# A gated, two-branch attention layer on one core: the down-projection as seven block products instead of eight

## The chip, the cores and the metric

The kernel runs on one core of one Trainium2 chip. The time is that of one execution on the device, in microseconds (us); it is given as the median of three runs, and one further execution was recorded by the profiler.

## The reference

One layer (DEPTH = 1) of 1024 positions by 1024 channels, all in float32. Two attention branches, gates and an output projection come first; none of them is touched here. The change lies in the channel mixing and in the last normalisation:

```python
h = _layer_norm(x) * (1.0 + sc2) + sh2
u = _causal_depthwise_conv(h @ w_up[l], conv_w[l], conv_b[l])   # (1024, 2 * 2816)
a, val = jnp.split(u, 2, axis=-1)
y = (jax.nn.silu(a) * val) @ w_down[l]                          # (1024, 2816) @ (2816, 1024)
x = _layer_norm(alpha * x + (1.0 + g2) * y, ln2_g[l], ln2_b[l])
```

## The kernel before

**Precision.** Each float32 operand of a large product is split in a high part, rounded to the multiplication format fp32r, and a low part, the rest. A product is then three matmuls: high by high, high by low, low by high. ScalarE (ACT) casts the high part, and GpSimd (POOL) or VectorE (DVE) subtracts to get the low part. So an operand of 128x512 costs a cast and a subtraction beside its loads.

**Up-projection** (`up(c)`, once for each of 22 blocks of 128 hidden channels). The up-projection is already done with seven block products instead of eight: the 1024 positions are two halves, the 1024 input channels two halves, and each block has one weight block of the gate and one of the value. Sums and differences of weights (`s1`, `s2`, `wt`, L1015, L1017, L727, on DVE) meet sums and differences of the input that were formed earlier; `product` (L741) issues 12 matmuls into a PSUM bank, and the results are combined by ACT copies and by DVE additions (`add`, L995). Some banks (`main`, `side`) are added to again by the next product after they have been read. The first eight blocks have two of their products done ahead of time (`early`, five products left); they alternate with later blocks in `order`. `conv` makes the causal convolution in PSUM (L976 on ACT, L978 twice on DVE), then SiLU (L981, ACT) and the product with the value (L983, DVE), which gives `y`, the block's 128 channels by 1024 positions. `stored()` at the next block's start writes `y` to the DRAM tensor `yd`.

**Down-projection.** The 1024 positions are taken in two halves of four row tiles; the 1024 output columns are two halves of 512. For a half of positions eight PSUM banks hold the sums (4 row tiles by 2 column halves), and for each of the 22 blocks `down` issues 4 x 2 x 3 matmuls. `load_g` fetches a half of `yd` (256 KB) and splits it (L1067 on ACT, L1068 on DVE; on POOL for the first three); `load_down` fetches 128 rows of `w_down` (512 KB) and splits them (L1061 on ACT, L1062 on POOL). The split weights of 16 blocks stay in SBUF for the second half of positions, those of six blocks are loaded and split again. The first three blocks (`FIRST`) are prepared in the up-projection's own buffers, before its memory is given over to the pool `dn`. In the second half the last six blocks (`LAST`) are taken row tile by row tile, so that a row tile is finished while the next ones are multiplied.

**Last normalisation.** `residual_2` multiplies a bank with `g2row` (`z`, L1120) and adds the scaled residual (L1121); `finish` takes the statistics (L115, L117 and some one-column instructions), normalises on ACT (L136), multiplies with `l2g` on DVE (L1127; on POOL for row tile 6), adds `l2b` on POOL (L1128) and stores. Row tile 7 is done in two halves on DVE alone (L1134, L1135), with no ACT and no POOL.

**Order.** The program is written as one stream; a scheduler places the instructions into the queues of the engines with its own model of time, waits included. Each engine then serves its queue strictly in order. Nearly all loads and stores are issued from one queue, that of SyncE (SP). Buffers of a pool are reused in turn: an instruction that writes a buffer waits for the last reader of what lay there.

Of the kernel before, what the change touches and what calls it, by code (L numbers as in the profile page):

```python
# [11 lines left out]
F32 = mybir.dt.float32  # L12
# [30 lines left out]
def body(ctx, tc, a, out):  # L43
# [41 lines left out]
    yd = dram.tile([NFF, P, S], F32, name="yd", tag="yd")  # L85
# [26 lines left out]
    def norm_scale(src, n=2):  # L112
        st = small.tile([P, n, 6], F32, name=nm("st"), tag=f"st{n}", bufs=4 if n == 2 else 1)
        for i in range(n):
            ve.bn_stats(out=st[:, i, :], in_=src[:, i * D // n : (i + 1) * D // n])  # L115
# [15 lines left out]
    def normalise(dst, src, on_act=False):  # L131
        mv, r = norm_scale(src)
        if on_act:
            b = small.tile([P, 1], F32, name=nm("nb"), tag="nb")
            ve.scalar_tensor_tensor(out=b, in0=mv[:, 0:1], scalar=-1.0, in1=r, op0=ALU.mult, op1=ALU.mult)
            se.activation(out=dst, in_=src, func=AF.Identity, scale=r, bias=b)  # L136
        else:
            ve.tensor_scalar(out=dst, in0=src, scalar1=mv[:, 0:1], scalar2=r, op0=ALU.subtract, op1=ALU.mult)
# [848 lines left out]
    def stored():  # L987
        while pending:
            c, ya = pending.pop()
            sy.dma_start(out=yd[c], in_=ya)  # L990
# [6 lines left out]
    def up(c):  # L997
# [60 lines left out]
    def load_down(dh, dl, c):  # L1058
        st = wp.tile([P, D], F32, name=nm("ws"), tag="ws")
        sy.dma_start(out=st, in_=a["w_down"][order[c]])  # L1060
        se.copy(out=dh, in_=st)  # L1061
        po.tensor_sub(out=dl, in0=st, in1=dh)  # L1062
        return dh, dl

    def load_g(st, gh, gl, c, half, eng):
        sy.dma_start(out=st, in_=yd[order[c], :, halves(half)])
        se.copy(out=gh, in_=st)  # L1067
        eng.tensor_sub(out=gl, in0=st, in1=gh)  # L1068
        return gh, gl

    def down(ps, t, g, d, start, stop, ns=(0, 1)):
        ts = slice(t * P, (t + 1) * P)
        for n in ns:
            pe.matmul(ps[n], g[0][:, ts], d[0][:, halves(n)], start=start, stop=False)  # L1074
            pe.matmul(ps[n], g[0][:, ts], d[1][:, halves(n)], start=False, stop=False)  # L1075
            pe.matmul(ps[n], g[1][:, ts], d[0][:, halves(n)], start=False, stop=stop)  # L1076

    def banks():
        return [[(mxt if t == 3 else mxp).tile([P, H], F32, name=nm("psd"), tag="tt" if t == 3 else "mm") for _ in range(2)]
                for t in range(4)]  # L1080

    ps = banks()
    firsts = []
    for c in range(FIRST):
        w = slot([P, 2, H], F32R)
        g = load_g(hbp.tile([P, H], F32, name=nm("gs"), tag="fs", bufs=2), w[:, 0], w[:, 1], c, 0, po)
        firsts.append((g, load_down(slot([P, D], F32R), slot([P, D], F32R), c)))
    stored()
    for c in range(FIRST):
        for t in range(4):  # L1090
            down(ps[t], t, *firsts[c], c == 0, False)
# [5 lines left out]
    with tc.tile_pool(name="dn", bufs=2, reuse_waits="tile") as dn:  # L1097
        downs = {}
        fixed = [FIRST + 2, FIRST + 3]

        def next_down(c):
            if c in fixed:
                dh, dl = [wp.tile([P, D], F32R, name=nm("dd"), tag=tag) for tag in ("wh", "wl")]
            else:
                d = dn.tile([P, 2, D], F32R, name=nm("dd"), tag="dd", bufs=KEEP)
                dh, dl = d[:, 0], d[:, 1]
            downs[c] = load_down(dh, dl, c)

        def next_g(c, half):
            return load_g(dn.tile([P, H], F32, name=nm("gs"), tag="gs", bufs=2),  # L1110
                          dn.tile([P, H], F32R, name=nm("gh"), tag="gh", bufs=LAST + 1),
                          dn.tile([P, H], F32R, name=nm("gl"), tag="gl", bufs=LAST + 1), c, half, ve)

        def residual_2(t, ps, w=H):
            y = dn.tile([P, D], F32, name=nm("yt"), tag="yt", bufs=4)
            sy.dma_start(out=y, in_=xd[t])
            for n in range(D // w):
                ns = slice(n * w, (n + 1) * w)
                z = dn.tile([P, w], F32, name=nm("z"), tag="z", bufs=2)
                ve.tensor_tensor(out=z, in0=ps[n * w // H][:, n * w % H : n * w % H + w], in1=g2row[:, ns], op=ALU.mult)  # L1120
                ve.scalar_tensor_tensor(out=y[:, ns], in0=y[:, ns], scalar=ALPHA, in1=z, op0=ALU.mult, op1=ALU.add)  # L1121
            return y

        def finish(t, y):
            if t < NT - 1:
                normalise(y, y, True)
                (po if t == NT - 2 else ve).tensor_tensor(out=y, in0=y, in1=l2g, op=ALU.mult)  # L1127
                po.tensor_tensor(out=y, in0=y, in1=l2b, op=ALU.add)  # L1128
# [8 lines left out]

        for c in range(FIRST, NFF):
            next_down(c)
            g = next_g(c, 0)  # L1140
            for t in range(4):
                down(ps[t], t, g, downs[c], False, c == NFF - 1)
        l2g = dn.tile([P, D], F32, name="l2g", tag="l2g", bufs=1)
        l2b = dn.tile([P, D], F32, name="l2b", tag="l2b", bufs=1)
        sy.dma_start(out=l2g, in_=a["ln2_g"].partition_broadcast(P))
        sy.dma_start(out=l2b, in_=a["ln2_b"].partition_broadcast(P))
        ys = [residual_2(t, ps[t]) for t in range(4)]
        ring = [c for c in range(FIRST, NFF) if c not in fixed]
        kept = ring[-KEEP:]
        again = list(range(FIRST)) + ring[:-KEEP]  # L1150
        turn = kept[: len(again)] + fixed + kept[len(again) : KEEP - LAST] + again + kept[KEEP - LAST :]
        ps = banks()
        for i, c in enumerate(turn[:-LAST]):
            if c in again:
                next_down(c)
            g = next_g(c, 1)
            for t in range(4):
                down(ps[t], t, g, downs[c], i == 0, False)
            if i < 4:
                finish(i, ys[i])  # L1160
        gs = [next_g(c, 1) for c in turn[-LAST:]]
        for t in range(4):
            for ns in ((0, 1),) if t < 3 else ((0,), (1,)):
                for i, c in enumerate(turn[-LAST:]):
                    down(ps[t], t, gs[i], downs[c], False, i == LAST - 1, ns)
            finish(4 + t, residual_2(4 + t, ps[t], H if t < 3 else H // 2))
# [64 lines left out]
```

## Time and profile before

| | |
|---|---|
| three runs | 1646.95, 1649.61, 1650.62 us; median 1649.61 |
| the profiled execution | 1647.35 us, of which the span from its first to its last instruction 1645.6 |
| TensorE (PE) busy | 1564.6 us, 95% of the span |
| VectorE (DVE) busy | 1078.8 us, 66% |
| ScalarE (ACT) busy | 780.1 us, 47% |
| GpSimd (POOL) busy | 540.5 us, 33% |
| mean granted TensorE clock | 0.982 of full speed |
| up-projection | until 1392 us |
| down-projection | 1392 to 1632 us |
| after the last matmul | to 1645.6 us |

Instructions are named by the kernel's line (L741), engine, operation and tiles, output before inputs (`psu<-hc,wx`). Busy time of PE is modelled and doesn't show how full its pipeline is. An idle time is put down to what ended it (`<-ACT gh L1067`). In the timeline, a row has its start, its length from the first start to the last end, the engine and line, and how many instructions are merged in it.

### The profile page before, as it was taken

The page shows a single profiled execution, that of the slowest core. Times are in us where ns is not written, and L with a number is a line of the kernel's source. Part 1 is how long each engine was busy: PE and PEld are TensorE (multiplying, and loading weights), DVE is VectorE, ACT ScalarE, POOL GpSimd, SP SyncE. Part 2 cuts the span into 40 slices and gives each one's busy share as a digit, 9 for nine tenths or more (in the row PEclk, how much of TensorE's full clock was granted, in tenths as well). Part 3 has the DMA queues.
Part 4 walks back from the last instruction along what each step waited for, and adds up shares of the span by engine and source line. Part 5 has one row for each costly group of instructions (what it writes and reads, how often), then busy time and mean ns, then how long its engine had stood idle before and what let it go on. Part 6 is the DMA issues. An engine that isn't in the chain of part 4 may idle for free. (4 is left out here: it accounts for less than half of the span.)

```text
span 1645.6 us, 21971 instructions
## 1 busy us (share of the span) xinstructions
PE 1564.6 (95%) x7821; PEld 1301.3 (79%) x7821; DVE 1078.8 (66%) x2189; ACT 780.1 (47%) x1380; POOL 540.5 (33%) x516
## 2 busy tenths in 40 slices
PE   6899999999999999999998969999999999999996
PEld 3788888889888888877876757788888888888885
DVE  6738776686677665537598795767766664554617
ACT  3547556655565555654245363444454454331311
POOL 1111213112322322222063544544444444550602
PEclk9999999999999999999998989999999999999998
DMA  9134432342252333247446245323332212761611
GB/s 348 43 95 120 139 91 77 114 129 65 77 167 84 103 96 122 72 163 245 153 161 236 97 159 165 116 97 119 113 101 97 77 71 90 246 215 45 204 40 51
DMA packets 81823, 205.80 MB, mean 125 GB/s; under 512 B 8561, under 2 KB 17329, under 8 KB 81713
## 3 DMA queue, kind: packets, MB, share of 16 engines
q1 hardware_dynamic: 77104, 197.49, 37.0%
q10 hardware_dynamic: 4608, 6.90, 1.1%
q8 instruction: 61, 1.00, 0.3%
q14 instruction: 50, 0.40, 0.1%
HBM read 157.14 MB, written 38.83 MB: 119 GB/s over the span
## 5 line engine op out<-in xcount | busy, mean ns | idle before, releaser
L98 POOL TENSOR_TENSOR wl<-ws,wh 128x1024 fp32r<-128x1024 f32 x54 | 133.0, 2466 | 320.1 <-ACT wh L97 293.6
L741 PE MATMUL psu<-hc,wx 128*128 128x512 f32 x804 | 194.9, 397 | 4.0 <-DVE u L995 4.0
L741 PEld LDWEIGHTS psu<-hc,wx 128*128 128x128 f32 x804 | 151.9, 189 | 41.4 <-DVE u L995 4.8
L978 DVE SCALAR_TENSOR_TENSOR pcv<-u,convp,pcv 128x1024 f32<-128x1024 f32 x88 | 113.0, 1284 | 48.2 <-ACT pcv L976 47.6
L1068 DVE TENSOR_TENSOR gl<-gs,gh 128x512 fp32r<-128x512 f32 x41 | 64.2, 1572 | 102.3 <-ACT gh L1067 94.5
L1074 PE MATMUL psd<-dd,gh 128*128 128x512 f32 x328 | 127.6, 389 | 0.0
L1075 PE MATMUL psd<-dd,gh 128*128 128x512 f32 x328 | 127.6, 389 | 0.0
L1076 PE MATMUL psd<-dd,gl 128*128 128x512 f32 x328 | 127.4, 389 | 0.0
L459 ACT ACTIVATE s<-s,mx 128x640 f32<-128x640 f32 (+7 forms) x128 | 94.6, 739 | 47.5 <-DVE mx L453 46.0
L498 ACT CAST pt<-pst 128x512 fp32r<-128x512 f32 (+1 forms) x192 | 82.4, 452 | 67.4 <-PE pst L494 63.4
L211 PE MATMUL psq<-h1h,wh 128*128 128x512 f32 x256 | 104.7, 410 | 2.0 <-DVE h1h L207 2.0
L211 PE MATMUL psg<-h1h,wh 128*128 128x512 f32 x256 | 103.9, 406 | 0.0
L212 PE MATMUL psq<-h1l,wh 128*128 128x512 f32 x256 | 101.1, 395 | 0.0
L213 PE MATMUL psq<-h1h,wl 128*128 128x512 f32 x256 | 100.9, 394 | 0.0
L499 DVE TENSOR_TENSOR pt<-pst,pt 128x512 fp32r<-128x512 f32 (+1 forms) x192 | 96.7, 517 | 5.9 <-ACT pt L498 4.0
L212 PE MATMUL psg<-h1l,wh 128*128 128x512 f32 x256 | 100.2, 392 | 0.0
L213 PE MATMUL psg<-h1h,wl 128*128 128x512 f32 x256 | 100.2, 391 | 0.0
L509 PE MATMUL pso<-pt,vs 128*128 128x256 f32 x608 | 92.0, 290 | 3.5 <-DVE o L514 1.7
L509 PEld LDWEIGHTS pso<-pt,vs 128*128 128x128 f32 x608 | 81.8, 191 | 12.9 <-ACT pt L498 4.0
L1062 POOL TENSOR_TENSOR dd<-ws,dd 128x1024 fp32r<-128x1024 f32 x25 | 62.5, 2504 | 89.3 <-ACT dd L1061 86.0
L97 ACT CAST wh<-ws 128x1024 fp32r<-128x1024 f32 x54 | 56.4, 1047 | 67.6 <-PE psq L212 20.6
L494 PE MATMUL pst<-ident,s 128*128 128x128 f32 x528 | 81.7, 273 | 7.1 <-DVE pt L499 3.7
(245 smaller groups left out, 4009.9 us busy)
## 6 DMA issues: line engine op xcount, KB each, us to landing
ws<-in_w_up SPq DMA_DIRECT2D x52, 512.0 KB, 3.4
wa<-in_w_ada SPq DMA_DIRECT2D x64, 256.0 KB, 3.1
ws<-in_w_down SPq DMA_DIRECT2D x28, 512.0 KB, 3.5
yd<-y SPq DMA_DIRECT2D x22, 512.0 KB, 3.0
gs<-yd SPq DMA_DIRECT2D x44, 256.0 KB, 3.5
wa<-in_w_ada SPq DMA_DIRECT2D x8, 1024.0 KB, 12.1
ws<-in_w_qk SPq DMA_DIRECT2D x16, 512.0 KB, 5.0
ws<-in_w_g SPq DMA_DIRECT2D x16, 512.0 KB, 3.7
```

Of the source, the lines that this page charges most:

```text
L98: po.tensor_sub(out=lo, in0=st, in1=hi)
L211: pe.matmul(ps, wh, xh, start=start, stop=False)
L212: pe.matmul(ps, wh, xl, start=False, stop=False)
L213: pe.matmul(ps, wl, xh, start=False, stop=stop)
L459: se.activation(out=st[:, 0:nk], in_=st[:, 0:nk], func=AF.Exp, scale=-1.0, bias=prev, accum_out=sm)
L499: ve.tensor_sub(out=dl, in0=src, in1=dh)
L509: pe.matmul(ps[:, 0:256], vs[:, j0 + j, :], pt[c][j // 4][:, j % 4, :], start=j == 0 and c == 0, stop=j == nj - 1 and c == 1)
L741: pe.matmul(ps, w[:, a_, k, :], h[k][b_], start=first, stop=k == 3 and a_ == 1, skip_group_check=on)
L978: ve.scalar_tensor_tensor(out=ps, in0=u[b][:, 2 - d : S + 2 - d], scalar=cp[:, 2 - d : 3 - d], in1=ps, op0=ALU.mult, op1=ALU.add)
L1074: pe.matmul(ps[n], g[0][:, ts], d[0][:, halves(n)], start=start, stop=False)
L1075: pe.matmul(ps[n], g[0][:, ts], d[1][:, halves(n)], start=False, stop=False)
L1076: pe.matmul(ps[n], g[1][:, ts], d[0][:, halves(n)], start=False, stop=stop)
```

## The change

The 22 blocks are taken as 11 pairs (two neighbours in `order`), so that the product has two halves of positions, two halves of the inner dimension (first and second block of each pair) and two halves of columns. Seven products replace the eight: their left operands are four blocks of `y` or sums of them, their right operands are blocks of `w_down` or sums of them.

- In the up-projection, `stored()` now waits for two blocks and forms the left operands of a pair with four DVE instructions of 128x512: `s3 = a11 - a21`, `a21 += a22` in place, `s2 = a21 - a11`, `s4 = a12 - s2`. It writes both `y` (512 KB each) to `yd` and three sums (256 KB each) to a new DRAM tensor `sd`. `y` gets three buffers instead of two, `p1` one instead of two, `mc` three instead of two.
- The down-projection runs the products in the order P1, P5, P6, P3, P2, P7, P4, each over the 11 pairs, on four row tiles and one column half, that is 12 matmuls per pair. P1, P6, P7 and P4 add to the same four PSUM banks (`bank_a`), P5 and P3 to four others (`bank_b`), which P2 then starts afresh. After P1, P5 and P6 ACT copies the banks to SBUF (`kept`); after P3, P2 and P7 DVE adds such a copy to the banks and forms the residual (`summed`, three instructions for each bank).
- `pair` loads both operands as 128x512 pieces of 256 KB (nine raw buffers). For P5, P6, P7 and P4 DVE forms a difference of weight blocks (two raw loads in P5 and P7). Both operands are then split by `parted`: cast on ACT, subtraction on DVE; GpSimd splits nothing. There are 20 buffers for split operands, two for each pair. Nothing split is kept from one product to another.
- The first four pairs of P1 are prepared in the up-projection's buffers (48 matmuls; before, three blocks with 72).
- The last eight pairs of P4 are taken row tile by row tile. All eight row tiles of the residual `xd` are loaded after P5's last pair has been asked for.
- Row tiles 0 to 3 are finished after P2, 4 to 7 with P4. The statistics of a row tile's right half are taken after P7. Row tile 6 is now finished like row tile 7, on DVE with no GpSimd; the others multiply with `l2g` on DVE and add `l2b` on GpSimd.

```diff
+    sd = dram.tile([NPAIR, 3, P, H], F32, name="sd", tag="sd")
...
     def stored():
-        while pending:
-            c, ya = pending.pop()
-            sy.dma_start(out=yd[c], in_=ya)
+        if len(pending) < 2:
+            return
+        (c, y0), (_, y1) = pending
...
+        ve.tensor_tensor(out=s3, in0=a11, in1=a21, op=ALU.subtract)
+        ve.tensor_tensor(out=a21, in0=a21, in1=a22, op=ALU.add)
+        ve.tensor_tensor(out=s2, in0=a21, in1=a11, op=ALU.subtract)
+        ve.tensor_tensor(out=s4, in0=a12, in1=s2, op=ALU.subtract)
+        sy.dma_start(out=yd[i, 0], in_=y0)
+        sy.dma_start(out=yd[i, 1], in_=y1)
+        for j, x in enumerate((s2, s3, s4)):
+            sy.dma_start(out=sd[i, j], in_=x)
...
+    products = "P1 P5 P6 P3 P2 P7 P4".split()
+    def a_src(p, i):
+        return {"P1": yd[i, 0, :, halves(0)], "P5": yd[i, 0, :, halves(1)], "P2": yd[i, 1, :, halves(0)],
+                "P4": yd[i, 1, :, halves(1)], "P6": sd[i, 0], "P7": sd[i, 1], "P3": sd[i, 2]}[p]
+    def parted(w, st):
+        se.copy(out=w[:, 0], in_=st)
+        ve.tensor_sub(out=w[:, 1], in0=st, in1=w[:, 0])
+        return w
...
+    for i in range(FIRST):
+        if i == FIRST - 1:
+            stored()
+        g = parted(slot([P, 2, H], F32R), loaded(hbp.tile([P, H], F32, name=nm("gs"), tag="fs", bufs=2), a_src("P1", i)))
+        d = parted(slot([P, 2, H], F32R), loaded(wp.tile([P, H], F32, name=nm("ws"), tag="ws"), b_src(i, 0, 0)))
...
+        def pair(p, i):
+            g, d = [dn.tile([P, 2, H], F32R, name=nm("op"), tag="op", bufs=20) for _ in range(2)]
+            parted(g, loaded(raw_tile(), a_src(p, i)))
+            if p == "P5":
+                x, y = loaded(raw_tile(), b_src(i, 0, 1)), loaded(raw_tile(), b_src(i, 0, 0))
+                sums[i] = dn.tile([P, H], F32, name=nm("t1"), tag=f"t{i}", bufs=1)
+                ve.tensor_tensor(out=sums[i], in0=x, in1=y, op=ALU.subtract)
+                st = sums[i]
+            elif p in ("P6", "P4"):
+                x = loaded(raw_tile(), b_src(i, 1, 1 if p == "P6" else 0))
+                ve.tensor_tensor(out=sums[i], in0=x, in1=sums[i], op=ALU.subtract)
+                st = sums[i]
+            elif p == "P7":
+                st, y = loaded(raw_tile(), b_src(i, 1, 1)), loaded(raw_tile(), b_src(i, 0, 1))
+                ve.tensor_tensor(out=st, in0=st, in1=y, op=ALU.subtract)
             else:
+                st = loaded(raw_tile(), b_src(i, *{"P1": (0, 0), "P3": (1, 1), "P2": (1, 0)}[p]))
+            parted(d, st)
+            return g, d
+        def residual_2(y, n, x):
+            ns = halves(n)
+            ve.tensor_tensor(out=x, in0=x, in1=g2row[:, ns], op=ALU.mult)
+            ve.scalar_tensor_tensor(out=y[:, ns], in0=y[:, ns], scalar=ALPHA, in1=x, op0=ALU.mult, op1=ALU.add)
+        def summed(y, n, x, ps):
+            ve.tensor_tensor(out=x, in0=ps, in1=x, op=ALU.add)
+            residual_2(y, n, x)
...
+        for p in products:
+            ps = bank_b if p in ("P5", "P3", "P2") else bank_a
+            fresh = p in ("P1", "P5", "P2")
+            steps = range(FIRST if p == "P1" else 0, NPAIR)
+            last = LAST if p == "P4" else 1
+            for i in steps[:-last]:
+                w = pair(p, i)
+                for t in range(4):
+                    down(ps, t, w, fresh and i == 0, False, not fresh)
+            ws = [pair(p, i) for i in steps[-last:]]
...
             for t in range(4):
+                for w in ws:
+                    down(ps, t, w, False, w is ws[-1], not fresh)
+                if p == "P4":
...
+                    ve.bn_stats(out=stats[t][:, 0, :], in_=y[:, n0])
+                    finish(4 + t, y, stats[t])
...
+                    elif p == "P2":
+                        summed(ys[t], 0, p1[t], ps[t])
+                        finish(t, ys[t])
+                    else:
+                        summed(ys[4 + t], 1, p5[t], ps[t])
+                        ve.bn_stats(out=stats[t][:, 1, :], in_=ys[4 + t][:, halves(1)])
```

More of the change, by code (lines that the diff above doesn't have):

```diff
@@ L110, in split_scaled, with norm_scale @@
         return dst
[L112 to L115, printed above, removed]
+    def norm_scale(src, n=2, st=None):
+        if st is None:
+            st = small.tile([P, n, 6], F32, name=nm("st"), tag=f"st{n}", bufs=4 if n == 2 else 1)
+            for i in range(n):
+                ve.bn_stats(out=st[:, i, :], in_=src[:, i * D // n : (i + 1) * D // n])
         mv = small.tile([P, 2], F32, name=nm("mv"), tag="mv")
@@ L1057, in body @@
     mxt_cm, mxt = opened(name="mxt2", bufs=2, space=PSUM)
[L1058 to L1069, printed above, removed]
@@ L1071, in down @@
-    def down(ps, t, g, d, start, stop, ns=(0, 1)):
-        ts = slice(t * P, (t + 1) * P)
[L1073 to L1080, printed above, removed]
@@ L1082, in body @@
-    ps = banks()
-    firsts = []
[L1084 to L1089, printed above, removed]
+    k0, k1 = order[0::2], order[1::2]
+    products = "P1 P5 P6 P3 P2 P7 P4".split()
+    def a_src(p, i):
+        return {"P1": yd[i, 0, :, halves(0)], "P5": yd[i, 0, :, halves(1)], "P2": yd[i, 1, :, halves(0)],
+                "P4": yd[i, 1, :, halves(1)], "P6": sd[i, 0], "P7": sd[i, 1], "P3": sd[i, 2]}[p]
@@ new lines, in b_src, with loaded, down @@
+    def b_src(i, r, c):
+        return a["w_down"][(k0, k1)[r][i]][:, halves(c)]
+    def parted(w, st):
+        se.copy(out=w[:, 0], in_=st)
+        ve.tensor_sub(out=w[:, 1], in0=st, in1=w[:, 0])
+        return w
+    def loaded(st, src):
+        sy.dma_start(out=st, in_=src)
+        return st
+    def down(ps, t, w, start, stop=False, on=False):
+        g, d = w
+        ts = slice(t * P, (t + 1) * P)
+        pe.matmul(ps[t], g[:, 0, ts], d[:, 0], start=start, stop=False, skip_group_check=on)
+        pe.matmul(ps[t], g[:, 0, ts], d[:, 1], start=False, stop=False, skip_group_check=on)
+        pe.matmul(ps[t], g[:, 1, ts], d[:, 0], start=False, stop=stop, skip_group_check=on)
@@ L1090, in body @@
+    for i in range(FIRST):
         for t in range(4):
-            down(ps[t], t, *firsts[c], c == 0, False)
+            down(bank_a, t, firsts[i], i == 0)
     hb_cm.__exit__(None, None, None)
@@ L1114, in residual_2 @@
[L1114 to L1122, printed above, removed]
@@ L1136, in finish @@
                     (sy, se)[n].dma_start(out=out[t * P : (t + 1) * P, ns], in_=y[:, ns])
-        for c in range(FIRST, NFF):
-            next_down(c)
-            g = next_g(c, 0)
-            for t in range(4):
[L1142 to L1160, printed above, removed]
```

88 lines of the change are left out of this document (56 added, 32 removed).

## The prediction

> **What bounds the kernel now.** First the page's head and the chain that ended last, then the table of stretches, then single rows of each stretch.
>
> ```profile
> span 1645.6 us, 21971 instructions
> PE 1564.6 (95%) x7821; PEld 1301.3 (79%) x7821; DVE 1078.8 (66%) x2189; ACT 780.1 (47%) x1380; POOL 540.5 (33%) x516
> PE psu L741 22%; PE psd L1074 5%; PE psd L1076 5%; PE psd L1075 4%; DVE yt L1121 1%; POOL wx L730 1%; DMA md<-mc 0%; POOL wl L730 0%; POOL wh L730 0%; DVE st L115 0%; DMA ws<-in_w_up 0%; DVE z L1120 0%; DVE s L1015 0%; DVE wt L727 0%; DVE u L995 0%
> ```
>
> The chain is TensorE's own work in the up- and the down-projection; VectorE is on it only at the very end. The stretches (busy us and instructions of PE, PEld, DVE, ACT, POOL, then granted clock, DMA share, GB/s):
>
> ```profile
> 1039.00:1074.00 35.00, 34.98 (x151) 28.37 (x152) 25.86 (x28) 16.16 (x23) 16.03 (x13) 1.00 0.32 106
> 1392.00:1632.00 240.00, 240.00 (x1061) 198.61 (x1059) 118.29 (x148) 63.94 (x85) 79.79 (x32) 1.00 0.40 135
> 1410.00:1450.00 40.00, 40.00 (x178) 33.12 (x177) 25.46 (x10) 16.41 (x21) 25.20 (x10) 1.00 0.78 267
> ```
>
> PE has no gap in either stage, at the full clock: the down-projection is worth the number of its matmuls. VectorE is half idle there (118 of 240) and three quarters busy in the up-projection (25.9 of 35). So a saving on PE counts in full until another engine is late, and VectorE is the one the change loads.
>
> **The matmuls.** One step of PE, from the first and the last matmul of the stage:
>
> ```profile
> L1074 PE MATMUL psd<-wh,wx x8: 389/389/393, 1392.8 to 1402.1; 128*128 128x512 f32 x8
> L1076 PE MATMUL psd<-dd,gl x328: 388/389/389, 1410.0 to 1631.9; 128*128 128x512 f32 x164
> ```
>
> Before: 2 halves x 22 blocks x 4 row tiles x 2 column halves x 3 passes = 1056, and (1631.9 - 1392.8) / 1055 = 0.2267 us each. After: 7 products x 11 pairs x 4 x 3 = 924. Saved 132 x 0.2267 = **-29.9 us**. A pair (12 matmuls) now lasts 2.72 us on PE.
>
> **VectorE in the down-projection.** Today GpSimd makes the weights' low parts (L1062) and VectorE only 41 low parts of activations. Afterwards VectorE does both for each pair, and in P5, P6, P7 and P4 also a difference of weights: 2 or 3 instructions of 128x512 a pair, besides three in each of 12 sums, four statistics and so on. Their price comes from the only place where VectorE runs packed today, where the first half's banks are emptied:
>
> ```profile
> 1508.27 1.28 DVE L1120 TENSOR_TENSOR z<-psd,g2row 128x512 f32<-128x512 f32 x2
> 1509.47 1.28 DVE L1121 SCALAR_TENSOR_TENSOR yt<-yt,z 128x512 f32<-128x512 f32 x2
> 1516.67 1.28 DVE L1121 SCALAR_TENSOR_TENSOR yt<-yt,z 128x512 f32<-128x512 f32 x2
> 1517.87 1.87 DVE L115 BATCH_NORM_STATS2 st<-yt 128x6 f32<-128x512 f32 x3
> ...
> 1526.49 2.71 DVE L1068 TENSOR_TENSOR gl<-gs,gh 128x512 fp32r<-128x512 f32 x1
> 1529.12 2.35 DVE L128 TENSOR_TENSOR r<-y,t 128x1 f32<-128x1 f32 x1
> 1539.63 5.68 DVE L1068 TENSOR_TENSOR gl<-gs,gh 128x512 fp32r<-128x512 f32 x2
> ```
>
> ```profile
> 1525.33 3.31 POOL L1128 TENSOR_TENSOR yt<-yt,l2b 128x1024 f32<-128x1024 f32 x1 [3.40 <-DVE yt L1127]
> 1528.61 2.84 POOL L1062 TENSOR_TENSOR dd<-ws,dd 128x1024 fp32r<-128x1024 f32 x1
> 1531.41 2.39 POOL L1128 TENSOR_TENSOR yt<-yt,l2b 128x1024 f32<-128x1024 f32 x1
> L1068 DVE TENSOR_TENSOR gl<-gs,gh x41: 678/693/2891, 1407.2 to 1594.7; 128x512 fp32r<-128x512 f32 x41
> L1067 ACT CAST gh<-gs x41: 601/621/624, 1406.5 to 1594.0; 128x512 fp32r<-128x512 f32 x41
> ```
>
> Two start every 1.20, so 0.60 us each. What reads two SBUF tensors also waits out any GpSimd instruction: the 128x1 product at 1529.12 took 2.35 and ended with GpSimd's at 1531.4. And the queue serves the program's order: the finishing of four row tiles ran from 1508.27 to 1539.6, with the low parts of the next activations squeezed to its gaps or behind it, though they were wanted.
>
> In P1, P5, P6 and P3 this is harmless: 1.2 or 1.8 us of VectorE for 2.72 of PE, and 20 operand buffers let it run 10 pairs ahead. ScalarE's two casts (1.24) and the 12 copies out of PSUM stay under the same 2.72. After P2 it isn't. Count from the end of P2's first bank. VectorE owes: P2's sums and the finishing of tiles 0 to 3, which is today's stretch of 31.4 less four evacuations (2.4) and the two low parts in it (1.2), 27.8; the 13 pairs that the buffers could not hold (22 of P7 and P4 less 9), 13 x 3 x 0.60 = 23.4; P7's sums with statistics, 16 x 0.60 = 9.6. In all 60.8. P4's last eight pairs are taken bank by bank, so PE wants the last of them after 9 + 132 + 36 + 21 = 198 matmuls, 44.9 us. PE waits the rest, **+15.9**. Ends: +6.3 if GpSimd's four additions of l2b (4 x 2.4) cost VectorE nothing, +22.7 if the 75 instructions of 512 columns above each take 0.69, the duration of a single one (the median below). I keep 15.9, since the stretch it rests on is measured with its waits.
>
> [...] The trace agrees with 0.69 for one alone, not for a packed run.
>
> **P3 to P2** share banks with no pause: PE returns to a bank 2.72 after leaving it, and three instructions a bank (1.8) against 0.68 on PE put the fourth bank's read up to 1.4 late. The pairs z, z, yt, yt above show that VectorE slips a ready read in front of a dependent step, so +0 to 1.4; I take **+1**. P7 to P4 lies inside the debt counted above.
>
> **The start of the stage.** Today:
>
> ```profile
> 1399.76 1.22 DVE L983 TENSOR_TENSOR y<-pcv,y 128x1024 f32<-128x1024 f32 x1
> 1401.01 0.33 SPq L990 DMA_DIRECT2D yd<-y  x1
> 1401.38 1.23 SPq L1066 DMA_DIRECT2D gs<-yd  x2
> 1406.54 1.27 ACT L1067 CAST gh<-gs 128x512 fp32r<-128x512 f32 x2 [7.55 <-DMA gs<-yd]
> 1407.19 1.35 DVE L1068 TENSOR_TENSOR gl<-gs,gh 128x512 fp32r<-128x512 f32 x2 [6.21 <-ACT gh L1067]
> yd<-y SPq DMA_DIRECT2D x22, 512.0 KB, 3.0
> ```
>
> PE is covered by 72 matmuls of the first three blocks, 16.3 us from 1392.8, and the next low part is there at 1407.9: one us to spare. Afterwards the cover is 48 matmuls, to 1403.7. SP's queue is in order, and the loads for the new pool stand behind the last stores, which now come as five and wait for three sums after y (1.8). So the pair comes at 1407.9 + 1.8 = 1409.7: **+6**. Ends: 0 if the loads stand ahead of the stores, 9 if a raw buffer lies on the y being stored (3.0 more, the landing of yd<-y).
>
> **The sums in the up-projection.** 44 instructions, 26 us of VectorE beside PE. Cover: what they delay. Behind them in the queue stand the additions that empty banks:
>
> ```profile
> 1248.20 8.56 PE L741 MATMUL psu<-hc,wx 128*128 128x512 f32 x36
> 1251.08 1.22 DVE L983 TENSOR_TENSOR y<-pcv,y 128x1024 f32<-128x1024 f32 x1
> 1251.95 1.30 POOL L730 TENSOR_TENSOR wx<-ws,wx 128x512 fp32r<-128x512 f32 x1 [1.50 <-ACT wx L729]
> 1252.22 0.68 DVE L995 TENSOR_TENSOR u<-psu,u 128x512 f32<-128x512 f32 x1
> ```
>
> The three products in the first row take 2.8 each; the third, from 1253.8, writes the bank that the L995 has read by 1252.9. Slack 0.9. One sum between (0.6) plus a GpSimd instruction waited out (up to 1.3, GpSimd being busy 16 of 35) costs 0 to 1.0; all three, 1.8 + 1.3 - 0.9 = 2.2. This place recurs for the 7 pairs followed by an early block: 0 to 15. The sums depend on each other, so other work slips between: 0.5 x 7, **+4** rounded up. The third y buffer and the single p1 cost nothing while stores land in 3 us against 33 a pair.
>
> **Loads.**
>
> ```profile
> gs<-yd SPq DMA_DIRECT2D x44, 256.0 KB, 3.5
> ws<-in_w_down SPq DMA_DIRECT2D x28, 512.0 KB, 3.5
> ```
>
> P5 and P7 fetch three 256 KB pieces a pair, 0.786 MB in 2.72 us, 289 GB/s. The stretch at 1410 moved 267 with a share of 0.78, so 342 is in reach and I take 0. The far end is a cap at 267: 2 x 29.9 x (289/267 - 1) = 4.9. [...] A piece lands 3.5 after its issue, and nine raw buffers, three pairs, cover 8 us of PE. On SP's queue xd (8 x 512 KB), l2g and l2b move ahead of P6's loads; they are wanted only after P3 and cost nothing unless they take the queue at the stage's start.
>
> **The end.** Today:
>
> ```profile
> 1633.06 4.60 DVE L1121 SCALAR_TENSOR_TENSOR yt<-yt,z 128x256 f32<-128x256 f32 x2
> 1632.56 2.34 POOL L1127 TENSOR_TENSOR yt<-yt,l2g 128x1024 f32<-128x1024 f32 x1 [5.77 <-ACT yt L136]
> 1634.98 2.40 POOL L1128 TENSOR_TENSOR yt<-yt,l2b 128x1024 f32<-128x1024 f32 x1
> 1640.74 1.42 DVE L1135 SCALAR_TENSOR_TENSOR yt<-yt,r,l2b 128x512 f32<-128x512 f32 x2
> ```
>
> 13.3 us from the last matmul (1631.9 + 0.4) to 1645.6, of which GpSimd's two instructions hold VectorE for nearly 4. Tile 6 leaves GpSimd, but tile 5's addition still falls on tile 6's chain and pushes it into tile 7's by some 2: **-2.3**, between -4 and +1.
>
> **Sum:** -29.9 + 15.9 + 1 + 6 + 4 + 0 - 2.3 = -5.3. The profiled run took 1647.35 (1.75 around its span), so 1642.0; it lay 2.3 under the median of 1649.61, so I say **1644.3**.
>
> **Rivals.**
> *VectorE postpones the finishing* of tiles 0 to 3 until the pairs are made: 60.8 less 20.6 is under 44.9, and no wait is left. -21.2: 1628. Against it: the order seen at 1508 to 1539.
> *The sums stop the up-projection* (slower): all three, with a GpSimd instruction, ahead of the L995 in the 7 places, 15 for 4, +5.7: 1655. It decides once they cost more than 1.3 each over the slack. For it: the slack of 0.9; against it: that dependent work is interleaved.
> [...]
> *Loads cap at 267 GB/s:* +4.9, -0.4: 1649.
>
> **Chances.** Forecast 0.48 (its own range 1637 to 1652), postponing 0.20, sums 0.17, 0.69 0.08, loads 0.07. A measurement tells some 0.2%, 3.3 us. Faster: 0.33 of the forecast's 0.48 and the 0.20. Same: 0.10 of it and most of the last two, 0.21. Slower: the sums, 0.05 of it and the rest, 0.26. The range goes from the postponing to the sums with the start at 9: 1627 to 1659.
>
> **What would show it.** PE's matmuls 132 fewer at the same 0.2267; PE idle behind VectorE's low parts in P7 and P4 (some 16 us), and for some 6 about 11 us after the first psd; PE's stretch to 1392 longer by about 4; the end 11 for 13.3. I am wrong if PE runs dense through P4 (postponing), or if its gaps lie in the up-projection or behind DMA.

## The result, and the profile after

The changed kernel took 1654.71 us in the median of 20 runs (1648.86 to 1661.31), the kernel before on the same chips 1649.78 (20 runs, 1646.95 to 1653.47). The ratio is 1.0028, 95% interval [1.0018, 1.0038]: slower by some 4.6 us by the ratio (4.9 between the medians), where 5.3 fewer were forecast. The range held the time, the direction was wrong. The profiled execution took 1651.2 us.

The page of the changed kernel: span, busy time of each engine, and the chain that ended last, by engine and by line.

```profile
span 1649.4 us, 22373 instructions
PE 1548.3 (94%) x7689; PEld 1280.6 (78%) x7689; DVE 1173.9 (71%) x2399; ACT 818.7 (50%) x1473; POOL 471.3 (29%) x483
PE 29%; DVE 4%; issue 1%; DMA 1%; ACT 1%; POOL 1%; DVEq 0%; SPq 0%; POOLq 0%; ACTq 0%
PE psu L743 17%; PE psd L1097 4%; PE psd L1098 4%; PE psd L1099 4%; DVE pcv L980 1%; DVE wt L729 1%; DMA ws<-in_w_up 1%; POOL wx L732 0%; ACT y L983 0%; DVE u L1012 0%; DVE op L1087 0%; DVE sc L1003 0%; DVE y L985 0%; DMA rw<-in_w_down 0%; DMA yd<-y 0%
```

PE has 132 matmuls fewer and is 16 us less busy, but the span grew. Scattered entries of VectorE have come into the chain: the taps of the convolution (`pcv`), a sum (`sc`), a low part (`op`). Where the time went is read from the first and last matmuls of each stage. First the up-projection before, then the up- and down-projection after:

```profile
L741 PE MATMUL psu<-ha,wh x132: 389/389/775, 931.6 to 1356.4; 128*128 128x512 f32 x132
L741 PE MATMUL psu<-hc,wx x804: 387/395/628, 1005.0 to 1392.5; 128*128 128x512 f32 x161
```

```profile
L743 PE MATMUL psu<-ha,wh x132: 387/389/775, 934.2 to 1364.6; 128*128 128x512 f32 x132
L743 PE MATMUL psu<-hc,wx x804: 392/396/628, 1007.5 to 1400.8; 128*128 128x512 f32 x161
L1099 PE MATMUL psd<-op,op x292: 387/389/628, 1419.0 to 1631.9; 128*128 128x512 f32 x146
```

The up-projection lasted 1392.5 - 931.6 = 460.9 before and 466.6 after; from its last matmul to the stage's last, 239.4 and 231.1; from there to the end, 13.7 and 17.5. What lies ahead of 934.2 is unchanged code; it began between 931.9 and 938.1 in the runs below, so its 2.6 is no effect of the change.

Inside the down-projection PE stood still three times; before, never. Rows of PE's weight loads (in brackets the idle time and what ended it), with one row of the up-projection:

```profile
1102.67 0.99 PEld L743 LDWEIGHTS psu<-hc,wx 128*128 128x128 f32 x5 [2.15 <-ACT u L1042]
1417.68 0.29 PEld L1097 LDWEIGHTS psd<-op,op 128*128 128x128 f32 x1 [5.97 <-ACT op L1086]
1473.30 0.30 PEld L1097 LDWEIGHTS psd<-op,op 128*128 128x128 f32 x2 [3.65 <-ACT op L1086]
1599.58 0.29 PEld L1097 LDWEIGHTS psd<-op,op 128*128 128x128 f32 x1 [6.40 <-ACT op L1086]
```

The matmul behind the last of these weight loads waited for a bank, and its row names VectorE:

```profile
1599.61 0.76 PE L1097 MATMUL psd<-op,op 128*128 128x512 f32 x1 [6.01 <-DVE p L1160]
```

The table of stretches around them (columns as in the prediction):

```profile
1401.00:1632.00 231.00, 216.22 (x925) 176.74 (x924) 177.91 (x304) 100.80 (x174) 15.87 (x4) 0.97 0.67 230
1417.70:1424.00 6.30, 6.30 (x14) 4.71 (x15) 5.08 (x8) 4.71 (x8) 0.00 (x0) 0.50 1.00 342
1440.00:1470.00 30.00, 30.00 (x133) 24.59 (x131) 13.17 (x21) 10.32 (x19) 0.00 (x0) 1.00 0.93 339
1599.60:1604.90 5.30, 5.29 (x13) 4.14 (x14) 5.30 (x8) 0.87 (x2) 1.50 (x1) 0.50 0.52 174
```

After the two long gaps the granted clock is 0.50 (half clock). From 1418.40 to 1424.09, and again from 1599.61 to 1605.14, PE got through 13 matmuls in 5.7 and 5.5 us, where 2.9 would do at full clock, so each gap costs 2.6 to 2.7 us more than itself. None of this was in the forecast. The last section shows waits of 3.04 and 3.36 us with half clock behind them.

The rows behind each of the four places follow. In the up-projection, at the block after a pair (VectorE, then ScalarE):

```profile
1092.36 0.68 DVE L1002 TENSOR_TENSOR sc<-y 128x512 f32<-128x512 f32 x1
1093.57 0.68 DVE L1003 TENSOR_TENSOR sc<-y,sc 128x512 f32<-128x512 f32 x1
1095.37 1.27 DVE L980 SCALAR_TENSOR_TENSOR pcv<-u,convp,pcv 128x1024 f32<-128x1024 f32 x1
1096.84 1.77 DVE L729 TENSOR_TENSOR wt<-ws,s 128x512 f32<-128x512 f32 x1 [0.20 <-POOL wx L732]
1098.53 1.28 DVE L980 SCALAR_TENSOR_TENSOR pcv<-u,convp,pcv 128x1024 f32<-128x1024 f32 x1
```

```profile
1099.84 1.03 ACT L983 ACTIVATE y<-pcv 128x1024 f32<-128x1024 f32 x1 [3.33 <-DVE pcv L980]
1100.90 1.21 ACT L978 ACTIVATE pcv<-u,convp 128x1024 f32<-128x1024 f32 x1
1102.05 0.57 ACT L1042 COPY u<-psu 128x512 f32<-128x512 f32 x1
```

The sums s2 and s4 (L1002, L1003) stand ahead of the convolution's taps (L980); ScalarE waits 3.33 for them, and in its queue the SiLU and the next convolution stand ahead of the copy (L1042) that empties the bank PE wants at 1100.5. Most of the delay reaches PE through ScalarE. The addition that the forecast watched (L995, now L1012) ends two new waits of 0.95, this one and one at 1339.39, and makes a wait at 1041.72 longer by 0.6:

```profile
1299.45 2.64 PEld L743 LDWEIGHTS psu<-hc,wx 128*128 128x128 f32 x12 [0.95 <-DVE u L1012]
```

At the start of the stage (SyncE's queue, then ScalarE):

```profile
1409.29 0.32 SPq L1005 DMA_DIRECT2D yd<-y  x1
1410.74 1.46 SPq L1007 DMA_DIRECT2D sd<-sc  x2
1413.24 0.32 SPq L1091 DMA_DIRECT2D rw<-yd  x1
1416.27 1.36 ACT L1086 CAST op<-rw 128x512 fp32r<-128x512 f32 x2 [10.91 <-DMA rw<-yd]
```

As forecast: the first load of the new pool stands behind the last stores. At P5 to P6:

```profile
1449.88 0.43 SPq L1192 DMA_DIRECT2D l2g<-in_ln_g  x1
1450.82 8.19 SPq L1091 DMA_DIRECT2D yt<-xd  x8
1460.04 0.32 SPq L1091 DMA_DIRECT2D rw<-sd  x1
1468.08 2.62 ACT L1150 COPY p<-psd 128x512 f32<-128x512 f32 x4 [12.00 <-PE psd L1099]
```

The residual's loads take the queue from 1449.9 to 1460, and with them the DMA is nearly full (339 GB/s at a share of 0.93 over the stretch from 1440 to 1470); P6's first operand is asked for 10 us late. Last, from the emptying of P2's first bank (1562.92) to the end (VectorE and GpSimd):

```profile
1562.92 1.28 DVE L1160 TENSOR_TENSOR p<-psd,p 128x512 f32<-128x512 f32 x2
1597.59 1.28 DVE L1136 TENSOR_TENSOR t<-rw,t 128x512 f32<-128x512 f32 x2
1598.79 1.27 DVE L1160 TENSOR_TENSOR p<-psd,p 128x512 f32<-128x512 f32 x2
1621.40 0.68 DVE L1087 TENSOR_TENSOR op<-t,op 128x512 fp32r<-128x512 f32 x1
1633.20 2.30 DVE L127 SCALAR_TENSOR_TENSOR t<-y,v 128x1 f32<-128x1 f32 x1
```

```profile
1594.13 6.97 POOL L1167 TENSOR_TENSOR yt<-yt,l2b 128x1024 f32<-128x1024 f32 x1 [5.04 <-DVE yt L1166]
1632.57 2.91 POOL L1167 TENSOR_TENSOR yt<-yt,l2b 128x1024 f32<-128x1024 f32 x1 [31.46 <-DVE nb L137]
```

P7 ended at 1593.2, but VectorE came to empty its bank at 1598.79, behind low parts and weight differences of P4; P4 adds to the same bank and had to wait. VectorE was done with low parts at 1622.1. In the tail GpSimd's two additions each held a one-column instruction of VectorE for 2.3 us.

### The profile page after: what moved, and what is told of

It is laid out like the page before. It is cut to its first block, busy times and chain, and to the rows that moved or that the text cites. A ratio compares the mean times of both kernels' runs of the same rounds, so it can differ in the third digit from the quotient of the medians.

```text
span 1649.4 us, 22373 instructions
## 1 busy us (share of the span) xinstructions
PE 1548.3 (94%) x7689; PEld 1280.6 (78%) x7689; DVE 1173.9 (71%) x2399; ACT 818.7 (50%) x1473; POOL 471.3 (29%) x483
## 5 line engine op out<-in xcount | busy, mean ns | idle before, releaser
L980 DVE SCALAR_TENSOR_TENSOR pcv<-u,convp,pcv 128x1024 f32<-128x1024 f32 x88 | 113.0, 1284 | 40.9 <-ACT pcv L978 40.0
L1097 PE MATMUL psd<-op,op 128*128 128x512 f32 x292 | 114.8, 398 | 14.8 <-ACT op L1086 8.8
L1098 PE MATMUL psd<-op,op 128*128 128x512 f32 x292 | 115.7, 397 | 0.0
L1099 PE MATMUL psd<-op,op 128*128 128x512 f32 x292 | 115.0, 396 | 0.0
L1087 DVE TENSOR_TENSOR op<-rw,op 128x512 fp32r<-128x512 f32 x113 | 74.5, 685 | 39.1 <-ACT op L1086 38.2
L1167 POOL TENSOR_TENSOR yt<-yt,l2b 128x1024 f32<-128x1024 f32 x6 | 21.6, 3601 | 243.1 <-DVE yt L1166 204.0
L1086 ACT CAST op<-rw 128x512 fp32r<-128x512 f32 x113 | 66.8, 620 | 48.6 <-PE psd L1099 20.1
```

The costliest lines, as they stand in the source:

```text
L980: ve.scalar_tensor_tensor(out=ps, in0=u[b][:, 2 - d : S + 2 - d], scalar=cp[:, 2 - d : 3 - d], in1=ps, op0=ALU.mult, op1=ALU.add)
L1097: pe.matmul(ps[t], g[:, 0, ts], d[:, 0], start=start, stop=False, skip_group_check=on)
L1098: pe.matmul(ps[t], g[:, 0, ts], d[:, 1], start=False, stop=False, skip_group_check=on)
L1099: pe.matmul(ps[t], g[:, 1, ts], d[:, 0], start=False, stop=stop, skip_group_check=on)
```

## The experiments

The theory was that VectorE's debt after P2 is the largest loss; rivals were the residual's loads, the operand sums in the up-projection, and the start. All lengths below are read as in the last section: up-projection, down-projection to its last matmul, rest of the span.

| kernel | up | down | rest | ratio to before, 95% |
|---|---|---|---|---|
| before | 460.9 | 239.4 | 13.7 | |
| changed | 466.6 | 231.1 | 17.5 | 1.0028 [1.0018, 1.0038] |
| l2b on VectorE | 469.2 | 231.9 | 13.1 | 1.0006 [0.9993, 1.0019] |
| VectorE work early | 468.8 | 233.7 | 12.7 | 1.0012 [0.9998, 1.0025] |
| five pairs first | 469.7 | 229.2 | 17.3 | 1.0016 [1.0003, 1.0028] |
| residual late | 470.2 | 225.8 | 17.0 | 1.0000 [0.9987, 1.0013] |
| no sums | 462.0 | 231.0 | 17.0 | 0.9992 [0.9982, 1.0003] |
| P4 in other banks | 472.1 | 233.4 | 20.1 | 1.0057 [1.0045, 1.0069] |
| the same, work early | 469.8 | 233.1 | 14.4 | 1.0017 [1.0007, 1.0028] |
| two sums on GpSimd | 468.7 | 233.8 | 17.6 | 1.0045 [1.0032, 1.0058] |
| before, tile 6 changed | 460.5 | 239.4 | 11.3 | 0.9984 [0.9970, 0.9998] |
| four edits together | 469.1 | 225.8 | 12.0 | 0.9965 [0.9951, 0.9979] |
| and sums weighted early | 469.8 | 217.4 | 11.3 | 0.9904 [0.9888, 0.9920] |
| and y's sums later | 463.9 | 217.0 | 11.4 | 0.9870 [0.9851, 0.9889] |

Nine of these kernels have the up-projection of the changed one, and it took 466.6 to 472.1 in them, 469.5 in the mean: the wait for the copy is now some 0.6 and now 2.15 us. The changed kernel's own profile is at the short end, 2.9 under the mean, which fits that it lies 3.5 under the median of its runs.

**l2b on VectorE.**

```diff
-                po.tensor_tensor(out=y, in0=y, in1=l2b, op=ALU.add)
+                ve.tensor_tensor(out=y, in0=y, in1=l2b, op=ALU.add)
```

> The changed kernel with the addition of l2b for row tiles 0 to 5 on VectorE instead of GpSimd. Theory (VectorE owes too much after P2, and GpSimd's additions are part of that debt because VectorE stands still while they run): each of the six additions held VectorE for 2.4 to 2.9 us and now costs it 1.22; four of them lie in the debt (-4 to -6, in the idle time of TensorE between P7 and P4 and in the tail), two in the tail behind the last matmul (17.1 us, to about 14.5). Expected: 7 us less than the changed kernel, about 1648, ratio to the kernel before 0.998 to 1.000. Rival (GpSimd's additions ran beside VectorE's work): six more VectorE instructions of 1.22, 5 to 7 us more, ratio 1.006.

0.22 points came back, 3.6 us, and six instructions more on VectorE made the kernel faster: GpSimd's additions did not run beside it, and in the changed kernel's tail two of them each held it for 2.3 us. The gain is in the tail (17.5 to 13.1). The gap between P7 and P4 only broke up, into 0.68, 3.04, 2.58, 0.63 and 1.56. Right in direction, about half in size.

**VectorE's work early.**

```diff
-            elif p in ("P6", "P4"):
-                x = loaded(raw_tile(), b_src(i, 1, 1 if p == "P6" else 0))
+            elif p == "P6":
+                x = loaded(raw_tile(), b_src(i, 1, 1))
...
+            elif p == "P4":
+                st = sums[i]
...
+            if p == "P3":
+                x = loaded(raw_tile(), b_src(i, 1, 0))
+                ve.tensor_tensor(out=sums[i], in0=x, in1=sums[i], op=ALU.subtract)
...
+                        ve.bn_stats(out=stats_0[t][:, 0, :], in_=ys[t][:, halves(0)])
+                        finish(t, ys[t], stats_0[t])
...
+                if p == "P3":
+                    for t in range(4):
+                        ve.bn_stats(out=stats_0[t][:, 1, :], in_=ys[t][:, halves(1)])
```

> The changed kernel with 9 us of VectorE's work taken from behind P2 to ahead of it, none left out: P4's 11 weight differences are formed while P3 runs (its VectorE has 1.8 us of work for 2.72 of TensorE then), and the statistics of the right halves of row tiles 0 to 3 behind P3. Theory (debt): TensorE's gap of 6.4 us between P7 and P4 goes, the half-clock stretch behind it too (about 3 us), and the last row tiles come apart, so the tail of 17.1 shrinks by 1 to 3. Expected -10 us, about 1645, ratio 0.997 (0.995 to 0.999). Rival (the gap at P7 to P4 is set by transfers or by the order of the queue, not by the amount of VectorE's work): the gap stays, no change within 2 us, ratio 1.002 to 1.004.

Only 2.6 us, and the gap stayed:

```profile
1602.98 0.29 PEld L1097 LDWEIGHTS psd<-op,op 128*128 128x128 f32 x1 [7.73 <-ACT op L1086]
```

VectorE filled the freed time with more low parts of P4, thirteen of them between 1592 and 1602, and all stand ahead of the emptying of P7's banks. The expectation that the amount of work sets this gap was wrong here: its order in the queue does too.

**Five pairs first** (`FIRST = 5` for 4).

> The changed kernel with five pairs of P1 prepared in the up-projection's buffers instead of four: the first matmuls of the down-projection cover 60 x 0.2267 = 13.6 us instead of 10.9. [...] Expected -5.7, about 1649, ratio 0.9995 (0.998 to 1.001). Rival (the new pool's first loads wait for the release of the buffers, which the fifth pair delays by its own 2.7 us): the gap stays at 6, no change, ratio 1.002 to 1.004.

The first gap became 3.85 and 0.54, and the clock still fell, for 3.4 us. Behind the second gap, 3.79 here, it fell for 3.4 us too, which it had not done in the changed kernel's profile. The down-projection gave 1.9, the ratio 0.12 points, 2.0 us of the 5.7 expected. The fifth pair's cover counts: the first wait was 5.97 in the changed kernel. The 5.7 also had some 3 us for a full clock behind this wait; the run shows half clock there.

**The residual late** (`if p == "P3":` for `"P5"` ahead of the loads of l2g, l2b and xd).

> The changed kernel with the loads of l2g, l2b and the eight row tiles of the residual asked for after P3's last pair instead of P5's. Theory (these loads, 5 MB in SyncE's queue, stand in front of P6's operands and made the gap of 3.65 us near 1470): the gap goes, -3.6, about 1651, ratio 1.000 (0.999 to 1.002), unless P2's loads now pay the same. Rival (the gap comes from ScalarE, whose copies out of PSUM after P5 stand in front of P6's casts): the gap stays, ratio 1.002 to 1.004. A second rival (the loads cost the same wherever they stand): the gap appears at P3 to P2 instead.

```profile
1460.00:1490.00 30.00, 30.00 (x134) 24.82 (x133) 26.23 (x43) 18.54 (x35) 0.00 (x0) 1.00 0.91 304
```

PE runs through the change from P5 to P6; the down-projection lasts 225.8 for 231.1, 0.28 points or 4.6 us. ScalarE's four copies are still there and cost nothing. The loads made the gap.

**No operand sums.** The operand sums are left out.

```diff
-        s2, s3, s4 = [hbp.tile([P, H], F32, name=nm("sc"), tag="mc", bufs=3) for _ in range(3)]
-        ve.tensor_tensor(out=s3, in0=a11, in1=a21, op=ALU.subtract)
-        ve.tensor_tensor(out=a21, in0=a21, in1=a22, op=ALU.add)
-        ve.tensor_tensor(out=s2, in0=a21, in1=a11, op=ALU.subtract)
-        ve.tensor_tensor(out=s4, in0=a12, in1=s2, op=ALU.subtract)
...
-        for j, x in enumerate((s2, s3, s4)):
+        for j, x in enumerate((a21, a11, a12)):
```

> The changed kernel without the four additions on y in the up-projection (the operand sums are left out: plain halves of y are stored in their place, with the same five stores). Over five profiles of kernels with the changed up-projection it lasted 466.6 to 470.2 us from the first product of h_11 to the last (468.9 in the mean) against 460.9 before. Theory (the sums s2 and s4 stand on VectorE ahead of an addition and of the convolution's taps; ScalarE's SiLU and convolution then stand ahead of the copy that empties a bank, and TensorE waits 0.5 to 2.15 us in each pair): the up-projection goes back to 461 to 462, -7, about 1647, ratio 0.9985 (0.997 to 1.000). Rival (the single p1 buffer, the third y or the stores hold it): it stays near 469, ratio 1.002 to 1.004.

```profile
L743 PE MATMUL psu<-ha,wh x132: 387/389/775, 936.8 to 1362.6; 128*128 128x512 f32 x132
L743 PE MATMUL psu<-hc,wx x804: 392/396/628, 1009.5 to 1398.8; 128*128 128x512 f32 x161
```

462.0, with the same five stores: 7.5 of the 8.6 us by which the up-projection had grown (469.5 less 460.9) go with the four sums. The three sums' tiles in `mc` go with them, but the last experiment keeps these tiles and comes to 463.9. So the rival is left with about 1 us.

**P4 in other banks.**

```diff
-            ps = bank_b if p in ("P5", "P3", "P2") else bank_a
-            fresh = p in ("P1", "P5", "P2")
+            ps = bank_b if p in ("P5", "P3", "P2", "P4") else bank_a
+            fresh = p in ("P1", "P5", "P2", "P4")
...
-                    ve.tensor_tensor(out=z, in0=ps[t], in1=g2row[:, n0], op=ALU.mult)
+                    ve.tensor_tensor(out=z, in0=ps[t], in1=u3[t], op=ALU.add)
+                    ve.tensor_tensor(out=z, in0=z, in1=g2row[:, n0], op=ALU.mult)
...
+                if p == "P7":
+                    u3 = kept("p1", ps)
```

> The changed kernel with P4 in the other four banks, started afresh; ScalarE copies P7's banks to SBUF and VectorE adds that copy to each bank of P4 (four additions more). Theory A (the gap of 6.4 us between P7 and P4 comes of the order in VectorE's queue: the emptying of P7's banks stands behind low parts of P4 that TensorE doesn't want yet, and P4 has to wait for the banks): the gap and the half clock behind it go, -6 to -9, the tail gains 0.6; about 1648, ratio 0.9985 to 0.9995. Theory B (VectorE simply owes too much after P2): TensorE waits as long, only later, behind low parts in P4; ratio 1.002 to 1.003.

```profile
1617.13 0.29 PEld L1098 LDWEIGHTS psd<-op,op 128*128 128x128 f32 x1 [6.88 <-DVE op L1087]
```

The gap moved into P4, as long as before, and now ends on a low part. So the bank alone was not the cause: with the banks apart, PE waits for VectorE's work. The four additions more cost in the tail (20.1 for 17.5), and the ratio, 1.0057, is worse than either theory gave.

**The same, with VectorE's work early** (both edits).

> The previous one with P4's 11 weight differences formed during P3 and the right-half statistics of row tiles 0 to 3 behind P3. Moving these 9 us alone left the gap between P7 and P4 at 7.7 us (0.9 more ahead of it) and shortened the tail from 17 to 12.7. Theory A: as with P4's banks alone, with the shorter tail besides: 1645, ratio 0.997. Theory B: the debt is now 15.9 - 9 less than the change had, and with the banks apart nothing else holds TensorE: gaps of 2 to 6 us in P4, ratio 0.998 to 1.000, and clearly under the kernel with the banks alone. If the gap is neither (transfers late), the ratio stays at 1.001.

1.0017 against 1.0057: with the banks apart, the 9 us moved bring 0.40 points, 6.6 us; the ratio is still above what either theory gave. By the profiles the gain lies in the tail (14.4 for 20.1); the down-projection stayed at 233. A gap of 6.71 remains, and this one is made by order again: the emptying of P7's banks (9.6 us from 1605.8) stands ahead of the low part that PE wants. So both hold: VectorE has more to do than PE gives it time for, and its queue puts the wrong work first.

**Two sums on GpSimd** (`po` for `ve` in s2 and s4).

> The changed kernel with two of the four additions on y (s2 and s4, the two that stand ahead of a bank's addition and the convolution) on GpSimd. Theory (it is the place in VectorE's queue that costs): the up-projection falls from 469 to 462 to 465, about 1650, ratio 0.999 to 1.001. [...]

No gain: 468.7. Other waits took their place (three of 2.05 to 2.28 before the copy L1030), and the first gap of the down-projection grew to 8.27: the first load was asked for 0.4 later, and the second operand landed another 2.1 later, for a reason that was not separated. The theory put the up-projection at 462 to 465; with both sums out of VectorE's queue it was no shorter.

**Before, with row tile 6 finished like row tile 7.**

```diff
-            if t < NT - 1:
+            if t < NT - 2:
                 normalise(y, y, True)
-                (po if t == NT - 2 else ve).tensor_tensor(out=y, in0=y, in1=l2g, op=ALU.mult)
+                ve.tensor_tensor(out=y, in0=y, in1=l2g, op=ALU.mult)
...
-                mv, r = norm_scale(y, 4)
+                mv, r = norm_scale(y, 4 if t == NT - 1 else 2)
```

> The kernel before with one part of the change alone: row tile 6 finished on VectorE in two halves like row tile 7, without GpSimd. Prediction's step: 13.3 us behind the last matmul become 11.0 (between -4 and +1), ratio 0.9985 (0.9975 to 1.0005). Rival (GpSimd's two instructions for tile 6 were the only cover that VectorE had there, so its own four instructions come on top): 13.3 become 14 to 15, ratio 1.0005 to 1.001.

The rest of the span fell from 13.7 to 11.3: -2.4 for -2.3 forecast, and 0.9984. This part of the change is a gain by itself, and in the changed kernel the late row tiles hide it.

**Four edits together** (the first four experiments).

> The changed kernel with four edits that were run alone before: l2b added on VectorE (1.0006 against 1.0028 of the changed kernel), P4's weight differences and the statistics of the right halves early (1.0012), five pairs prepared in the up-projection's buffers (1.0016), the residual loaded after P3's pairs (1.0000). If they act in different places the gains add, -0.22 -0.16 -0.12 -0.28 per cent: ratio 0.995, about 1642. If the first two pay for the same thing (both shortened the tail from 17 to 13), 0.9966. If the whole is held by the operand sums in the up-projection (7 us) alone, 1.0000 or above.

0.9965, as where the first two pay for the same thing: they share the tail (12.0), and the other two add in full.

**The kept sums weighted early.** The residual is loaded after P6's pairs here.

```diff
         def summed(y, n, x, ps):
-            ve.tensor_tensor(out=x, in0=ps, in1=x, op=ALU.add)
-            residual_2(y, n, x)
+            ve.tensor_tensor(out=x, in0=ps, in1=g2row[:, halves(n)], op=ALU.mult)
+            ve.tensor_tensor(out=y[:, halves(n)], in0=y[:, halves(n)], in1=x, op=ALU.add)
...
+            if p == "P3":
+                for t in range(4):
+                    residual_2(ys[t], 0, p1[t])
+                    residual_2(ys[t], 1, u2[t])
+                    residual_2(ys[4 + t], 1, p5[t])
```

> The previous kernel with two changes: the kept copies of P1, P5 and P6 are multiplied with g2row and added to the scaled residual while P6 and P3 run, so that behind P3, P2 and P7 each bank costs VectorE two instructions instead of three; and the residual is loaded after P6's pairs. Theory (VectorE's debt after P2): 8 x 0.6 = 4.8 us fewer between P2 and the last pair of P4, -2 to -5 against the previous kernel, ratio 0.992 to 0.994. Rival (by now transfers or the order of the queue hold P4): no change against the previous kernel.

0.9904 against 0.9965, 10 us for the 2 to 5 expected. The down-projection is 217.4, with no gap over 1.3 behind the first one. There is no half clock behind P7 either: the mean clock of the down-projection is 0.99, and the 3.4 us of half clock behind the first gap, 4.18 here, are left. How much of the 10 is the other place of the loads was not separated.

**The sums of y later in the program.**

```diff
-        stored()
         u = next(turns)
...
         conv(c, 1, y, u)
+        stored()
         pending.append((c, y))
```

> The previous kernel with the four additions on y put behind the next block's convolution in the program, so that the addition that empties a bank goes ahead of s2 in VectorE's queue, 0.6 us earlier, and the second one after the first tap of the convolution. Theory (it is the delay of the convolution by s2 and s4 that reaches ScalarE's copies): the convolution still stands behind s4, so only 1 to 3 of the 7 to 9 us come back: 0.9985 of the previous kernel. Rival (any order that keeps the four additions in that place costs the same): no change.

Here VectorE and ScalarE at the same place as in the rows of the changed kernel:

```profile
1088.59 0.69 DVE L1012 TENSOR_TENSOR u<-psu,u 128x512 f32<-128x512 f32 x1
1089.18 1.19 DVE L1002 TENSOR_TENSOR sc<-y 128x512 f32<-128x512 f32 x1
1091.50 1.27 DVE L980 SCALAR_TENSOR_TENSOR pcv<-u,convp,pcv 128x1024 f32<-128x1024 f32 x1
1093.29 1.27 DVE L980 SCALAR_TENSOR_TENSOR pcv<-u,convp,pcv 128x1024 f32<-128x1024 f32 x1
```

```profile
1094.60 1.02 ACT L983 ACTIVATE y<-pcv 128x1024 f32<-128x1024 f32 x1 [0.79 <-DVE pcv L980]
1097.17 0.58 ACT L1041 COPY u<-psu 128x512 f32<-128x512 f32 x1
```

The addition goes ahead of s2, and between the two taps stands an addition of 0.6 instead of the weight difference (L729, 1.77) that waited for GpSimd. The SiLU now comes 6.0 us behind the addition instead of 6.9, and 4.6 behind the start of the product on `ha` instead of 7.6. The up-projection fell to 463.9 with all four sums in it, the ratio from 0.9904 to 0.9870: 5.6 us for the 1 to 3 expected. This version beats both kernels, 1626.9 us in the median against 1650.25 for the kernel before beside it.

## Why the prediction was wrong

By its own steps; the miss is 1654.7 - 1644.3 = 10.4 us. Gaps and half clock are taken here from matmul start to matmul start, less 0.2267 for each step, so that nothing is counted twice (a gap between weight loads comes out 0.2 to 0.3 longer).

| step | forecast | shown | by |
|---|---|---|---|
| matmuls | -29.9 | -29.9 | 924 of 0.2267 |
| sums in the up-projection | +4 | +8.6 | mean of nine profiles less 460.9; 7.5 of it gone without the sums |
| start of the stage | +6 | +8.9 | 1411.75 to 1424.09, 15 steps: waits 6.2, half clock 2.7 |
| loads | 0 | +3.8 | 1469.69 to 1474.37, 4 steps; 4.6 by ratio when moved |
| P3 to P2 | +1 | 0 | no gap there |
| VectorE's debt | +15.9 | +15.0 | 1593.21 to 1605.14, 14 steps: wait 6.2, half clock 2.6; rest of the span 17.5 less 11.3 |
| end | -2.3 | -2.4 | the edit alone on the kernel before |
| sum | -5.3 | +4.0 | measured +4.6 |

Three terms failed, by 4.6, 2.9 and 3.8 us and all to the same side.

*"They are wanted only after P3 and cost nothing unless they take the queue at the stage's start."* This step asked when xd is wanted, and not what stands behind it. The loads moved ahead of P6's operands in an ordered queue, and with them the DMA had little to spare (339 GB/s, share 0.93); 10 us of queue cost 3.8 (5.4 in six other profiles, where half clock followed).

*"So other work slips between: 0.5 x 7, +4."* The size was wrong, and most of the way too: the slack of 0.9 was taken at the additions, and two waits of 0.95 did come there, but the larger part of the sums' delay went through the convolution and ScalarE's queue to a copy. The rival that the sums stop the up-projection, 15 us, was further off on the other side.

*"So the pair comes at 1407.9 + 1.8 = 1409.7: +6."* The waits were 6.2, as forecast. What the step lacked is the half clock behind them, which no stretch of the stage before shows, because PE had no such gap there. The kernel before does show it in the first 85 us of its up-projection, so the prediction's "no gap in either stage, at the full clock" does not hold there: behind a wait of 3.36 at 1010.89 its clock was 0.50.

```profile
1008.85:1012.26 3.41, 1.37 (x6) 1.15 (x7) 3.41 (x4) 1.70 (x4) 3.41 (x3) 1.00 0.00 0
1012.26:1015.68 3.42, 3.42 (x10) 2.63 (x9) 0.26 (x1) 0.83 (x2) 3.42 (x4) 0.50 0.47 141
```

The largest term, the matmuls, was right. The debt came out at 15.0 by size (VectorE's packed work ran from 1562.9 to 1622.1, 59.2 us, for the 60.8 counted), but not as one wait of PE: the scheduler interleaved P4's last eight pairs across row tiles, so that PE waited 6.2 and three row tiles were finished close together, and the rest came in the tail. That the sizes agree so well is in part luck: 2.6 of the 15.0 are half clock, which the step did not have. That the debt is real shows where banks and work were moved apart: 6.6 us for 9 moved, most of it in the tail. That the place of the gap is set by the queue's order shows in the early work alone, which brought 2.6 and left the gap.

The rivals: postponing didn't occur, since VectorE finished row tiles 0 to 3 ahead of P4's low parts. The 0.69 for each VectorE instruction, the upper end of the debt, didn't either: the row at 1597.59 has two in 1.28, so 0.60 apart, as before. Loads reached 339 GB/s over the stretch from 1440 to 1470, so the cap at 267 falls. That VectorE waits out any GpSimd instruction holds in the kernel before: of its sums, differences and products of two SBUF tensors, 61 began while a GpSimd instruction of the same kind had 0.3 us or more to run, and all 61 ended after it. In the changed kernel that is so for 53 of 60; the other seven took 0.68 each while GpSimd's addition at 1594.13 took 6.97.

## What to carry to other kernels

When a transfer is moved to an earlier place in an ordered queue, price it by what then stands behind it and by the bandwidth left at that time, and not by when its data are wanted; here 10 us of queue cost 3.8. When work is added to an engine with slack, follow it through every queue that its delay passes to the matmul engine; here the up-projection with the same four sums was 8.6 us longer than before in one order and 3.0 in another. A product saved on the matmul engine comes back only if the other engines' work is spread so that it keeps up at each hand-over: the same seven products gave 1.0028 and 0.9870.

## What the hardware showed that was not expected

A gap of PE's costs more than its length: after 5.97 and 6.40 us the granted clock was 0.50 for 6.8 us. The length alone does not decide it. A wait of 3.65 left the clock at 1.00 in the changed kernel and brought 3.4 us of half clock in six others; 4.18 (the kept sums weighted early) brought 3.4 and 4.15 (the sums of y later) brought 6.8. In the up-projection a wait of 3.36 at 1010.89 in the kernel before and one of 3.04 at 1013.04 in the changed kernel had 3.4 us of half clock behind them.

What separates the two in the profiles of both kernels is how much of one stretch of the clock's grid the wait fills. The drops begin and end on a grid of 3.41 us. Cut along it, the two profiles have 384 stretches at full clock between 940 and 1630 us. By the rows of its matmuls, whose ends are modelled, PE was busy for less than 41% of the time in seven of them, and behind each of these the next one ran at 0.50; behind the others, with 47% or more, none did. The stretch from 1008.85 of the kernel before, shown above, had 1.37 of 3.41, or 40%; the wait of 3.65 in the changed kernel fell across two stretches with 49% and 57%, and the clock stayed at 1.00:

```profile
1468.41:1471.82 3.41, 1.67 (x8) 1.05 (x6) 0.57 (x1) 2.54 (x5) 0.00 (x0) 1.00 1.05 386
1471.82:1475.24 3.42, 1.94 (x7) 1.33 (x8) 3.28 (x7) 2.18 (x4) 0.00 (x0) 1.00 0.87 295
```

The same instructions in the same order took 466.6 to 472.1 us in the up-projection. At six places the wait for ScalarE's copy is under 0.5, between 0.5 and 0.8, or 2.15 us, and which of them differs from profile to profile; the kernel before had no wait over 0.45 there.
